# A transformer trunk in float32: the MLP as one loop over both matrices, or as two stages with seven block products for the first

## The chip, the cores and the metric
One of the cores of a Trainium2 chip runs the kernel; nothing else runs beside it. The metric is device time of one execution in microseconds (us). The engines named below are PE (TensorE, matmuls), DVE (VectorE), ACT (ScalarE), POOL (GpSimd), and SP, on whose queue most transfers between DRAM and the core's SBUF memory are issued. Matmul results arrive in PSUM, which has eight banks of 128 x 512 float32.

## The reference
Two layers over 1024 latent tokens and 256 context tokens, 1024 features wide. Each layer: norm and modulation, three mixers (attention, Fourier, long convolution), one output projection, and then an MLP, which alone the change touches (with the projection before it):

```
x = x + g1 * heads_out(att_x, px, hy, w_out[l])
x = x + g2 * sq_relu_mlp(modulate(rms_norm(x, norm2_g[l]), sh2, sc2), w_mlp1[l], w_mlp2[l])
...
def sq_relu_mlp(h, w1, w2):
    return jnp.square(jax.nn.relu(h @ w1)) @ w2
```

`w1` is 1024 x 4096 and `w2` 4096 x 1024. Layer 0 does this for the context tokens too, with the same weights; layer 1 for the latents alone. Shift, scale and gate of layer 1 come from a product of a vector with a 1024 x 6144 matrix (`wmod`).

## The kernel before
Activations lie with features on the 128 partitions and tokens along the free axis, so x is eight tiles `xT` of 128 x 1024 (and `xC` of 128 x 256 for the context). Tokens are worked in chunks: 512, 512 and, in layer 0, 256 of the context.

Every float32 operand is cut into a high part (a cast on ACT) and a low part (the difference), and a product is three matmuls into one PSUM bank, high x high, high x low, low x high (`mm3`, lines 137 to 140). Weights come in raw tiles of 128 x 1024 (512 KB, `wload`, lines 122 to 128, into a ring of three to seven slots) and are cut by `wsplit` (lines 130 to 135): cast on ACT (L133), subtraction on POOL (L134). The parts `wh` and `wl` have two buffers each. Activations are cut by `split_sb` (L147, L148): cast on ACT, subtraction on DVE or, where it is asked for, POOL.

The order of the work: the program names the operations in sequence, each engine keeps its own queue, and background generators (`spawn(rate, gen)`) are advanced by `tick()` in the loops. A scheduler then reorders what is independent, so the order on an engine is not the text's.

After the attention the output projection runs as two calls of `half_k`: weights of four contraction tiles at a time, output tiles in four groups `mg` of two, and each PSUM result added onto x by `resid` (L1117, DVE reads PSUM and x). The second call goes chunk by chunk, and in layer 1 the last chunk is split into two of 256. As a chunk of x becomes final, its squares are summed (L199 on ACT, L201 on DVE), `rstd_diag` (L218, L219) and `rstd_rows` (L225 on PE, L227) turn the sum into a row, the norm's factor in every partition, and `norm_gen` makes the scaled and shifted operand's parts `hh` and `hl` (L243 to L245).

`mlp` then alternates: for each of eight groups `hc`, four weight tiles of `w1` times all chunks, relu and square (L1179 on ACT, L1180 on DVE), the parts `uh` and `ul` kept in SBUF, and then `half_k` with `w2` onto x. Beside layer 0's MLP `late_modulation` loads the last 48 tiles of layer 1's `wmod` and runs 64 dot products over 128 x 1024 on DVE (L161), spread by a rate of 0.45 per tick.

## Time and profile before

| what | value |
|---|---|
| time, three runs | 3266.49 us median (3265.97, 3266.49, 3275.97) |
| profiled execution, span from first to last instruction | 3268.1 us |
| PE busy | 3096.4 us, 16238 matmuls, 95 % of the span |
| PE weight loads, beside the matmuls | 2584.0 us, 79 % |
| DVE busy | 1830.7 us, 56 % |
| ACT busy | 1204.9 us, 37 % |
| POOL busy | 1049.0 us, 32 % |
| mean granted clock of PE | 0.978 of full |
| DMA | 326 MB, mean 100 GB/s |

The times and the profile are of different executions. For the profiled one only the span is known, which lies 1.6 us above the median. Busy matmul time is modelled at its ends, and neighbours overlap, so the price of one matmul is read from how many fit into a stretch, not from a mean duration. A wait is put down to the event that came last.

### The profile page before, as it was taken

The numbers are of one execution on the slowest core, as the hardware profiler recorded it, in microseconds if no ns is written. First come the engines' busy times: TensorE is split into PE (matmuls) and PEld (weight loads), VectorE is DVE, ScalarE is ACT, GpSimd is POOL, SyncE is SP. The second block draws the span as 40 slices with busy tenths as digits, with TensorE's granted clock in tenths as the row PEclk, the third lists the DMA queues.
The fourth block names the chain that finished last, engine by engine and source line by source line (L and its number), as shares of the span: only waits on it lengthen the run. The fifth ranks groups of instructions, "written<-read, shape, count | busy, mean of one in ns | idle before, by whom it ended". The sixth has DMA issues, their size and how long they took to land. (4 is left out here: it accounts for less than half of the span.)

```text
span 3268.1 us, 41676 instructions
## 1 busy us (share of the span) xinstructions
PE 3096.4 (95%) x16238; PEld 2584.0 (79%) x16238; DVE 1830.7 (56%) x2943; ACT 1204.9 (37%) x2167; POOL 1049.0 (32%) x676
## 2 busy tenths in 40 slices
PE   5999998999999999999999999998998999999997
PEld 1787886887778888888887887787877788888886
DVE  7985679886664444332226535779867322222226
ACT  4324475674331112112214424576654222222113
POOL 6334337542411111111113224347434222222223
PEclk8999998999999999999999998999999999999999
DMA  6454662434222232221113224653242111111113
GB/s 238 157 187 120 200 179 80 128 91 148 84 72 84 91 103 91 78 71 38 35 39 123 94 86 131 218 135 81 68 166 90 39 52 46 46 51 46 51 47 110
DMA packets 121036, 326.29 MB, mean 100 GB/s; under 512 B 32838, under 2 KB 44263, under 8 KB 120584
## 3 DMA queue, kind: packets, MB, share of 16 engines
q1 hardware_dynamic: 107832, 281.88, 27.7%
q0 software_dynamic: 9504, 34.67, 3.5%
q10 hardware_dynamic: 3504, 7.08, 0.6%
q8 instruction: 128, 2.10, 0.3%
q14 instruction: 68, 0.56, 0.1%
HBM read 270.11 MB, written 53.48 MB: 99 GB/s over the span
## 5 line engine op out<-in xcount | busy, mean ns | idle before, releaser
L134 POOL TENSOR_TENSOR wl<-wr,wh 128x1024 fp32r<-128x1024 f32 (+1 forms) x214 | 519.2, 2427 | 1641.8 <-ACT wh L133 1623.9
L133 ACT CAST wh<-wr 128x1024 fp32r<-128x1024 f32 (+1 forms) x214 | 221.5, 1035 | 962.0 <-PE pso L139 680.2
L140 PE MATMUL pso<-uh,wl 128*128 128x512 f32 (+1 forms) x1312 | 484.1, 369 | 4.2 <-POOL wl L134 4.2
L138 PE MATMUL pso<-uh,wh 128*128 128x512 f32 (+1 forms) x1312 | 487.5, 372 | 0.6 <-ACT wh L133 0.6
L1117 DVE SCALAR_TENSOR_TENSOR xT<-pso,modc,xT 128x512 f32<-128x512 f32 (+1 forms) x336 | 241.8, 722 | 438.4 <-PE pso L140 438.4
L138 PE MATMUL psm<-hh,wh 128*128 128x512 f32 (+1 forms) x1280 | 477.4, 374 | 4.3 <-ACT hh L244 4.2
L139 PE MATMUL pso<-ul,wh 128*128 128x512 f32 (+1 forms) x1312 | 480.7, 366 | 0.0
L140 PE MATMUL psm<-hh,wl 128*128 128x512 f32 (+1 forms) x1280 | 472.9, 370 | 3.5 <-POOL wl L134 3.5
L139 PE MATMUL psm<-hl,wh 128*128 128x512 f32 (+1 forms) x1280 | 474.9, 371 | 0.5 <-DVE hl L245 0.4
L1180 DVE SCALAR_TENSOR_TENSOR rl<-psm,rl 128x256 f32<-128x256 f32 (+1 forms) x160 | 101.7, 636 | 460.0 <-ACT rl L1179 459.9
L140 PEld LDWEIGHTS pso<-uh,wl 128*128 128x128 f32 x1312 | 247.8, 189 | 51.5 <-POOL wl L134 5.1
L139 PEld LDWEIGHTS pso<-ul,wh 128*128 128x128 f32 x1312 | 249.5, 190 | 45.2 <-issue 0.5
L138 PEld LDWEIGHTS pso<-uh,wh 128*128 128x128 f32 x1312 | 248.0, 189 | 44.5 <-ACT wh L133 0.8
L138 PEld LDWEIGHTS psm<-hh,wh 128*128 128x128 f32 x1280 | 241.7, 189 | 49.0 <-ACT hh L244 6.5
L140 PEld LDWEIGHTS psm<-hh,wl 128*128 128x128 f32 x1280 | 241.5, 189 | 47.9 <-POOL wl L134 3.9
L139 PEld LDWEIGHTS psm<-hl,wh 128*128 128x128 f32 x1280 | 241.6, 189 | 43.9 <-DVE hl L245 2.5
L1017 POOL TENSOR_SCALAR p<-p,st 128x1280 f32<-128x1280 f32 (+1 forms) x144 | 182.8, 1269 | 268.0 <-DVE st L1012 122.4
L144 DVE TENSOR_TENSOR pt<-pst,pt 128x512 fp32r<-128x512 f32 x328 | 214.4, 680 | 11.7 <-ACT pt L143 10.5
L143 ACT CAST pt<-pst 128x512 fp32r<-128x512 f32 x328 | 181.8, 589 | 86.3 <-PE pst L1038 68.2
L139 PE MATMUL psi<-hl,wh 128*128 128x512 f32 (+1 forms) x536 | 198.4, 370 | 5.8 <-POOL hl L241 3.4
L138 PE MATMUL psi<-hh,wh 128*128 128x512 f32 (+1 forms) x536 | 200.9, 376 | 1.8 <-ACT hh L244 1.1
L140 PE MATMUL psi<-hh,wl 128*128 128x512 f32 (+1 forms) x536 | 197.2, 368 | 3.2 <-POOL wl L134 3.2
(338 smaller groups left out, 6121.0 us busy)
## 6 DMA issues: line engine op xcount, KB each, us to landing
wr<-w SPq DMA_DIRECT2D x144, 512.0 KB, 3.5
wr<-wmod SPq DMA_DIRECT2D x64, 512.0 KB, 3.3
tb<-ftab POOLq DMA_DIRECT2D x34, 512.0 KB, 4.7
wm<-wmod SPq DMA_DIRECT2D x32, 512.0 KB, 3.6
wr<-wout SPq DMA_DIRECT2D x32, 512.0 KB, 3.6
wr<-win SPq DMA_DIRECT2D x26, 512.0 KB, 3.3
d_qk<-qk SPq DMA_DIRECT2D x18, 640.0 KB, 5.3
qk<-d_qk SPq DMA_DIRECT2D x18, 640.0 KB, 6.2
```

The lines of the kernel that those rows point to most:

```text
L133: S.copy(hi[:, :n], t[:, :n])
L134: G.tensor_tensor(lo[:, :n], t[:, :n], hi[:, :n].bitcast(F32), op=ALU.subtract)
L138: T.matmul(ps, lhsT=lh, rhs=rh, start=first, stop=False)
L139: T.matmul(ps, lhsT=lh, rhs=rl, start=False, stop=False)
L140: T.matmul(ps, lhsT=ll, rhs=rh, start=False, stop=last)
L143: S.copy(hi, ps)
L144: V.tensor_tensor(lo, ps, hi.bitcast(F32), op=ALU.subtract)
L1017: G.tensor_scalar(pr, pr, st[:, 5:6], 1.0, op0=ALU.mult, op1=ALU.mult)
L1117: V.scalar_tensor_tensor(x, ps[:, : c1 - c0], g, x, op0=ALU.mult, op1=ALU.add)
L1180: V.scalar_tensor_tensor(r[:, :n], ps[:, :n], 0.0, r[:, :n], op0=ALU.max, op1=ALU.mult)
```

## The change
The MLP becomes two stages, `up` and `down`, with the activations u = relu(.)^2 in DRAM (`d_u`) between them.

In `up` the latents' first matrix is worked as 2 x 2 blocks: the weights of two tiles A1 and A2 (a11, a12, a21, a22, half a tile each), the tokens' two halves and the two halves of the features. Seven products of four contraction tiles replace eight. Their token operands are b11, b21 (first half of the tokens), b22 and the four sums t1 to t4, made once a layer by `norm_blocks`; their weight operands are A1, `r41` (its halves a11 + a12 - a21 - a22 and a21 + a22), `r32` (a21 + a22 - a11 and a11 - a21) and half of A2, made for each of 16 periods j. Results are joined on DVE, passed through relu and square on ACT and stored. `top` makes the first two products p1 and p2, which need the first half of the tokens alone: for the first four (layer 0) or five (layer 1) periods they are made ahead, with their sum parked in DRAM (`d_s1`), while the second half's operands are made. The context keeps eight plain products per tile.

In `down` the tiles of u are loaded, cut again (low part on POOL) and multiplied with `w2` by `half_k` as before. x is stored to `d_x2` after the projection and loaded back in `down`. Layer 1's last chunk of the projection is one of 512. The late modulation starts inside `down`, from its second group, at a rate of 2.2.

```diff
+AHEAD = 4, 5
...
-        def mlp(l, xT, h, pool, psp, last_passes):
...
+            def second(acc):
+                yield
+                r = yield from rows(acc)
+                V.tensor_tensor(sh4, modc[:, l, 0, 3 * ND + 4 : 3 * ND + 8], modc[:, l, 0, 3 * ND : 3 * ND + 4], op=ALU.subtract)
+                for k in range(4):
+                    scaled(4 + k, xs1[4 + k], r)
+                    parts("b22", k, 4 + k, xs1[4 + k])
+                    if k % 2:
+                        yield
+                for k in range(4):
+                    scaled(k, xs1[k], r)
+                    t = nt("t1")
+                    V.tensor_tensor(t, xs1[k], xs0[k], op=ALU.subtract)
+                    split_sb(*ops["t1"][k], t, G)
+                    yield
+                    t3 = nt("t3")
+                    V.scalar_tensor_tensor(t3, xs1[4 + k], sh4[:, k : k + 1], xs1[k], op0=ALU.add, op1=ALU.subtract)
+                    split_sb(*ops["t3"][k], t3, G)
+                    t2 = nt("t2")
+                    V.scalar_tensor_tensor(t2, xs1[4 + k], shift(4 + k), t, op0=ALU.add, op1=ALU.subtract)
+                    split_sb(*ops["t2"][k], t2, G)
+                    yield
+                    t4 = nt("t4")
+                    V.scalar_tensor_tensor(t4, xs0[4 + k], shift(4 + k), t2, op0=ALU.add, op1=ALU.subtract)
+                    split_sb(*ops["t4"][k], t4, V)
...
+        def up(l, ops, hx, opening, psp, chain):
+            def prod(w, at, name):
+                ps = psp.tile([128, 512], F32, tag="ps", name="psm")
+                for k in range(4):
+                    ks = slice(at + k * 128, at + k * 128 + 128)
+                    mm3(ps, w[0][:, ks], w[1][:, ks], *ops[name][k], k == 0, k == 3)
+                return ps
...
+            def block(m, t0, x, y):
+                c = room("c")
+                V.tensor_tensor(c, x, y, op=ALU.add)
+                S.activation(c, c, AF.Relu)
+                out(c, m, t0)
...
+            def top(j, raw):
+                w = wsplit(raw, 1024)
+                p1 = prod(w, 0, "b11")
+                p2 = prod(w, 512, "b21")
+                s1 = room("s1")
+                S.copy(s1, p1)
+                block(2 * j, 0, s1, p2)
+                context(w, 2 * j)
+                return s1
+            for g in chain[:-1]:
+                drain(g)
+            for j in range(AHEAD[l]):
+                nc.sync.dma_start(out=d_s1[j], in_=top(j, wload(a["w1"][l, 2 * j], 1024)))
+                for _ in range(4):
+                    tick()
+            drain(chain[-1])
+            for j in range(16):
+                A1, A2 = (wload(a["w1"][l, 2 * j + u], 1024) for u in range(2))
+                a11, a12, a21, a22 = A1[:, :512], A1[:, 512:], A2[:, :512], A2[:, 512:]
+                if j < AHEAD[l]:
+                    s1 = room("s1")
+                    nc.sync.dma_start(out=s1, in_=d_s1[j])
+                else:
+                    s1 = top(j, A1)
+                r41 = wroom()
+                G.tensor_tensor(r41[:, 512:], a21, a22, op=ALU.add)
+                V.tensor_tensor(r41[:, :512], a11, a12, op=ALU.add)
+                V.tensor_tensor(r41[:, :512], r41[:, :512], r41[:, 512:], op=ALU.subtract)
+                w = wsplit(r41, 1024)
+                if j == 0:
+                    pool = opening()
+                    slots((pool, "wr2", 4))
+                    ring["at"] = 2
+                r32 = wroom()
+                V.tensor_tensor(r32[:, 512:], r41[:, 512:], a11, op=ALU.subtract)
+                V.tensor_tensor(r32[:, :512], a11, a21, op=ALU.subtract)
+                p3 = prod(w, 0, "b22")
+                p5 = prod(w, 512, "t1")
+                tick()
+                w = wsplit(r32, 1024)
+                p7 = prod(w, 0, "t3")
+                p6 = prod(w, 512, "t2")
+                V.tensor_tensor(s1, s1, p6, op=ALU.add)
+                u3 = room("u3")
+                V.tensor_tensor(u3, s1, p7, op=ALU.add)
+                V.tensor_tensor(s1, s1, p5, op=ALU.add)
+                block(2 * j + 1, 512, u3, p5)
+                block(2 * j, 512, s1, p3)
+                tick()
+                w = wsplit(A2, 1024)
+                p4 = prod(w, 512, "t4")
+                block(2 * j + 1, 0, u3, p4)
+                context(w, 2 * j + 1)
+                tick()
+        def down(l, xT, chunks, pools, psp, late, last_passes):
+            te = chunks[-1][1] if chunks[-1][1] > SEQ else SEQ
+            def load(hc, us):
+                for j in range(4):
+                    u = {c0: tuple(pools[hc % 2].tile([128, c1 - c0], F32R, tag=f"u{c1 - c0}", bufs=16 if c1 - c0 == 512 else 8,
+                                             name=f"u{x}") for x in "hl") for c0, c1, _ in chunks}
+                    w = pools[0].tile([128, TT], F32, tag="ur", bufs=3, name="ur")
+                    nc.sync.dma_start(out=w[:, :te], in_=d_u[hc * 4 + j][:, :te])
+                    for c0, (hi, lo) in sorted(u.items()):
+                        split_sb(hi, lo, w[:, c0 : c0 + hi.shape[1]], G)
+                    us.append(u)
+                    yield
...
+            us = [[] for _ in range(8)]
+            drain(load(0, us[0]))
+            back = load_back()
+            next(back)
+            spawn(1, back)
+            for hc in range(7):
+                g = load(hc + 1, us[hc + 1])
+                spawn(1, g)
+                if hc == 1:
+                    spawn(2.2, late)
+                half_k(l, 5, a["w2"][l, hc], us[hc], chunks, xT, psp)
+                drain(g)
+            now_ = us[7]
+            last_passes(now_)
...
-            h2 = new_h(PM, cself if last else cself[2:] + cself[:2])
-            crow = PM.tile([128, 2, 1024], F32, name="crow")
-            norms = spawn(1)
-            halves = [(c0, c1, cc, hs, todo) for cc, ce, hs, todo in h2
-                      for c0, c1 in (((cc, cc + 256), (cc + 256, ce)) if last and cc else ((cc, ce),))]
-            for i, (c0, c1, cc, hs, todo) in enumerate(halves):
-                acc, dg = (crow[:, i % 2, u * 512 : u * 512 + c1 - c0] for u in range(2))
-                part = [tuple(x[:, c0 - cc : c1 - cc] for x in p) for p in hs]
-                half_k(l, 2, a["wout"][l, 0], cat2, [(c0, c1, cc)], xT, psp,
-                       after=sums_by(acc, [xcol(xT, j, c0, c1) for j in range(ND)]))
-                g = norm_gen(l, 1, xT, c0, c1, part, acc, dg)
-                todo.append(g)
-                spawn(1, g)
+            hx = None if last else new_h(PM, CHUNKS[2:])[0][2]
+            acc = [PM.tile([128, 512], F32, name=f"nacc{i}") for i in range(2)]
+            dg = PM.tile([128, 512], F32, name="ndg")
+            sh4 = PM.tile([128, 4], F32, name="sh4")
+            norms = norm_blocks(l, [x[0][:, :512] for x in xT], [x[0][:, 512:] for x in xT], ops, acc, dg, sh4)
+            todo = ([] if last else [(CHUNKS[2], acc[1], norm_gen(l, 1, xT, SEQ, TT, hx, acc[1][:, :CTX], dg[:, :CTX]))]) + \
+                [(CHUNKS[i], acc[i], norms[i]) for i in range(2)]
+            for (c0, c1), ac, g in todo:
+                add = sums_by(ac[:, : c1 - c0], [xcol(xT, j, c0, c1) for j in range(ND)])
+
+                def after(mg, c0=c0, c1=c1, add=add):
+                    add(mg)
+                    for j in (2 * mg, 2 * mg + 1):
+                        nc.sync.dma_start(out=d_x2[j][:, c0:c1], in_=xcol(xT, j, c0, c1))
+
+                half_k(l, 2, a["wout"][l, 0], cat2, [(c0, c1, c0)], xT, psp, after=after)
+                spawn(2, g)
...
+            up(l, ops, hx, opening, psp, [g for _, _, g in todo])
+            slots()
+            wctx.close()
+            PMc.close()
+            xT = alloc_x(xctx, l + 1 if not last else DEPTH)
+            uctx = ExitStack()
...
                 if not last:
                     def late_modulation():
-                        for _ in range(3):
-                            yield
+                        crow = pools[0].tile([128, 2, 1024], F32, name="crow")
                         load_crow(crow)
                         yield from modulation(1, crow, (1, 0, 2, 4, 3, 5), lambda s: (0, 1) if s < 2 else (0,))
 
-                    spawn(0.45, late_modulation())
+                    late = late_modulation()
...
-                mlp(l, xT, h2, pool, psp, last_passes)
+                slots((pools[0], "wr2", 2))
+                down(l, xT, chs, pools, psp, late, last_passes)
```

The order in three places. First DVE, layer 1, where the normed operands are made. Before, each tile of the first half's operand takes a scaled row (L243) and a low part (L245):

```order
L243 SCALAR_TENSOR_TENSOR ht_22445<-xT0_21552,gsc_63,rstd_22443 128x512
L243 SCALAR_TENSOR_TENSOR ht_22449<-xT1_21553,gsc_63,rstd_22443 128x512
L243 SCALAR_TENSOR_TENSOR ht_22453<-xT2_21554,gsc_63,rstd_22443 128x512
L245 SCALAR_TENSOR_TENSOR hl0_0_22082<-ht_22445,modc_62,hh0_0_22081 128x512
L245 SCALAR_TENSOR_TENSOR hl0_1_22084<-ht_22449,modc_62,hh0_1_22083 128x512
L243 SCALAR_TENSOR_TENSOR ht_22457<-xT3_21555,gsc_63,rstd_22443 128x512
L245 SCALAR_TENSOR_TENSOR hl0_2_22086<-ht_22453,modc_62,hh0_2_22085 128x512
```

Now, in the second half (L1177 scaled row, L1182 low part of a shifted operand, L1211 to L1222 the sums, L155 their low parts, L1250 the joining of two products, `xT0` to `xT7` the tiles of x):

```order
L1177 SCALAR_TENSOR_TENSOR xT0_22182<-xT0_22182,gsc_63,rstd_23201 128x512
L1177 SCALAR_TENSOR_TENSOR xT1_22183<-xT1_22183,gsc_63,rstd_23201 128x512
L1211 TENSOR_TENSOR t1_23217<-xT0_22182 128x512
L1182 SCALAR_TENSOR_TENSOR b22l3_23117<-xT7_22189,modc_62,b22h3_23116 128x512
L1215 SCALAR_TENSOR_TENSOR t3_23221<-xT4_22186,sh4_22733,xT0_22182 128x512
L1218 SCALAR_TENSOR_TENSOR t2_23225<-xT4_22186,modc_62,t1_23217 128x512
L1177 SCALAR_TENSOR_TENSOR xT2_22184<-xT2_22184,gsc_63,rstd_23201 128x512
L1222 SCALAR_TENSOR_TENSOR t4_23229<-xT4_22186,modc_62,t2_23225 128x512
L1177 SCALAR_TENSOR_TENSOR xT3_22185<-xT3_22185,gsc_63,rstd_23201 128x512
L1250 TENSOR_TENSOR c_23267<-s1_23265,psm_23252 128x512
L1211 TENSOR_TENSOR t1_23274<-xT1_22183 128x512
L155 TENSOR_TENSOR t4l0_23143<-t4_23229,t4h0_23142 128x512
```

For two tiles of features there are eight operations, each with two inputs in SBUF, where four stood, and among them the joins of the first periods (L1250, one input in PSUM).

Second, POOL in layer 1's first stage. Before, one row per weight tile:

```order
L134 TENSOR_TENSOR wl_24911<-wr_24908,wh_24910 128x1024
L134 TENSOR_TENSOR wl_24981<-wr_24978,wh_24980 128x1024
```

Now, in a period (L141 the low part of a weight pair, of A1, r41, r32 and A2 in turn; L1290 the sum a21 + a22, a period ahead):

```order
L1290 TENSOR_TENSOR wr_24178<-wr_24139 128x512
L141 TENSOR_TENSOR wl_23998<-wr_23993,wh_23997 128x1024
L141 TENSOR_TENSOR wl_24039<-wr_24034,wh_24038 128x1024
L141 TENSOR_TENSOR wl_24072<-wr_24042,wh_24071 128x1024
L141 TENSOR_TENSOR wl_24116<-wr_23995,wh_24115 128x1024
L1290 TENSOR_TENSOR wr_24322<-wr_24283 128x512
```

For two weight tiles there are four weight pairs and one addition.

Third, SP's queue at the end of layer 0's first stage. Before, at that place in the MLP, only weights are loaded:

```order
L127 DMA wr_9786<-w1 128x1024
L127 DMA wr_9824<-wmod 128x1024
L127 DMA wr_9898<-wmod 128x1024
L127 DMA wr_9904<-w1 128x1024
L127 DMA wr_9974<-wmod 128x1024
```

Now (L1246 stores of u, L1329 its loads, L1339 x loaded back; `d_u31` is the last tile of u, `d_u1` to `d_u3` belong to the first group of the second stage):

```order
L1246 DMA d_u31_134<-c_12310 128x512
L1329 DMA ur_12409<-d_u0_103 128x1280
L1246 DMA d_u30_133<-c_12315 128x512
L1246 DMA d_u31_134<-c_12337 128x512
L1246 DMA d_u31_134<-c_12367 128x256
L1329 DMA ur_12423<-d_u1_104 128x1280
L1329 DMA ur_12437<-d_u2_105 128x1280
L1329 DMA ur_12451<-d_u3_106 128x1280
L1339 DMA xT0_12381<-d_x20_95 128x1024
```

and some rows further on

```order
L1329 DMA ur_12599<-d_u6_109 128x1280
L1329 DMA ur_12647<-d_u7_110 128x1280
L134 DMA wr_12711<-w2 128x1024
L134 DMA wr_12801<-w2 128x1024
```

The loads of u1 to u3 stand behind the context's last store, and two of the first group's weight tiles behind the second group's tiles of u.

## Rows read from the trace of the kernel before

**Rows 1.** The head of the page: the span, each engine's busy time (share of the span, instructions), and PE and its granted clock in 40 equal slices, each digit in tenths.
```profile
span 3268.1 us, 41676 instructions
...
PE 3096.4 (95%) x16238; PEld 2584.0 (79%) x16238; DVE 1830.7 (56%) x2943; ACT 1204.9 (37%) x2167; POOL 1049.0 (32%) x676
...
PE   5999998999999999999999999998998999999997
...
PEclk8999998999999999999999998999999999999999
```

**Rows 2.** Busy time of each engine in stretches: stretch in us, its length, then busy us of PE, of its weight loads, of DVE, ACT and POOL (with instructions), the mean granted clock of PE, the busy share of the DMA engines, GB/s. 820 to 960 is layer 0's step from the output projection to the MLP and 2480 to 2560 layer 1's; 960 to 1740 lies in layer 0's MLP and 2600 to 3200 in layer 1's.
```profile
820.00:840.00 20.00, 19.51 (x133) 17.76 (x131) 8.78 (x13) 4.56 (x7) 6.04 (x4) 1.00 0.27 79
840.00:860.00 20.00, 17.41 (x87) 14.36 (x87) 14.54 (x15) 8.75 (x14) 10.06 (x5) 1.00 0.32 106
...
880.00:900.00 20.00, 18.00 (x98) 14.80 (x97) 16.93 (x23) 8.32 (x14) 7.43 (x4) 1.00 0.28 83
900.00:920.00 20.00, 17.20 (x74) 12.45 (x74) 17.50 (x30) 11.43 (x21) 0.00 (x0) 0.94 0.23 73
920.00:940.00 20.00, 18.00 (x97) 14.83 (x96) 12.29 (x18) 12.16 (x17) 5.17 (x2) 0.97 0.16 56
960.00:1740.00 780.00, 780.00 (x4033) 663.48 (x4032) 297.47 (x471) 146.34 (x224) 138.05 (x56) 1.00 0.22 71
2480.00:2500.00 20.00, 18.37 (x134) 16.72 (x133) 17.24 (x20) 10.51 (x16) 11.84 (x6) 1.00 0.37 111
2500.00:2520.00 20.00, 12.37 (x86) 11.67 (x85) 19.41 (x23) 10.97 (x18) 8.31 (x4) 0.88 0.35 111
2520.00:2540.00 20.00, 14.15 (x54) 11.44 (x54) 15.79 (x35) 8.66 (x20) 2.34 (x1) 0.78 0.12 42
2540.00:2560.00 20.00, 18.40 (x72) 14.66 (x73) 10.86 (x22) 8.37 (x16) 4.82 (x2) 0.91 0.12 33
2600.00:3200.00 600.00, 600.00 (x2599) 488.33 (x2598) 166.06 (x216) 121.92 (x166) 130.57 (x55) 1.00 0.16 48
```

**Rows 3.** PE's waits between 2480 and 2570 us: what waited, for which engine's operation; us in total, times, longest. L225 spreads the norm's row (from L219 on DVE) over the partitions.
```profile
PE psn L225 <- DVE crow L219: 10.3, 2, 8.6
PE pso L140 <- POOL wl L134: 3.6, 4, 2.0
```

**Rows 4.** The page's costliest groups: the first of the three matmuls of a product in the MLP's first matrix; busy us, mean ns of one, idle before it.
```profile
L138 PE MATMUL psm<-hh,wh 128*128 128x512 f32 (+1 forms) x1280 | 477.4, 374 | 4.3 <-ACT hh L244 4.2
```

**Rows 5.** DVE in time order around the same step of layer 1: start us, us, line and operation, out<-in, in brackets the idle time before and its cause. A row with x3 is three operations in a row. L201 adds squares (two SBUF tiles), L1117 adds a PSUM tile onto x, L243 scales x by the norm's row (two SBUF tiles).
```profile
2482.50 0.69 DVE L201 TENSOR_TENSOR crow<-crow,sq 128x512 f32<-128x512 f32 x1 [0.76 <-ACT sq L199]
...
2484.23 0.48 DVE L1117 SCALAR_TENSOR_TENSOR xT<-pso,modc,xT 128x256 f32<-128x256 f32 x1 [0.37 <-PE pso L140]
2484.63 2.06 DVE L201 TENSOR_TENSOR crow<-crow,sq 128x512 f32<-128x512 f32 x1
...
2491.59 2.33 DVE L201 TENSOR_TENSOR crow<-crow,sq 128x256 f32<-128x256 f32 x1 [0.48 <-ACT sq L199]
...
2502.45 2.08 DVE L243 SCALAR_TENSOR_TENSOR ht<-xT,gsc,rstd 128x512 f32<-128x512 f32 x3
...
2505.77 2.84 DVE L243 SCALAR_TENSOR_TENSOR ht<-xT,gsc,rstd 128x512 f32<-128x512 f32 x1
```

**Rows 6.** POOL's groups by shape: the low part of a weight pair, and of a 512-wide tile; count, busy us, mean ns, idle before.
```profile
L134 POOL TENSOR_TENSOR wl<-wr,wh 128x1024 fp32r<-128x1024 f32 x204 | 502.4, 2464 | 1630.1 <-ACT wh L133 1612.2 <-PE pso L140 17.8
...
L148 POOL TENSOR_TENSOR heho<-eo,heho 128x512 fp32r<-128x512 f32 x18 | 25.3, 1405 | 24.7 <-ACT heho L147 24.7
```

**Rows 7.** POOL in time order, same columns as rows 5.
```profile
2483.74 2.39 POOL L134 TENSOR_TENSOR wl<-wr,wh 128x1024 fp32r<-128x1024 f32 x1 [3.21 <-ACT wh L133]
...
2491.27 2.37 POOL L134 TENSOR_TENSOR wl<-wr,wh 128x1024 fp32r<-128x1024 f32 x1 [2.20 <-ACT wh L133]
...
2505.63 2.43 POOL L134 TENSOR_TENSOR wl<-wr,wh 128x1024 fp32r<-128x1024 f32 x1 [4.88 <-ACT wh L133]
```

**Rows 8.** ACT's groups by shape: the high part of a weight pair, and of a 512-wide tile.
```profile
L133 ACT CAST wh<-wr 128x1024 fp32r<-128x1024 f32 x204 | 214.0, 1049 | 952.3 <-PE pso L139 680.2 <-PE psm L139 190.6 <-PE psi L139 36.1
...
L147 ACT CAST uh<-rl 128x512 fp32r<-128x512 f32 x128 | 79.4, 621 | 94.0 <-DVE rl L1180 94.0
```

**Rows 9.** PE in time order, three matmuls of the output projection that waited for the low part of a weight pair, in brackets for how long.
```profile
2486.19 0.39 PE L140 MATMUL pso<-cat,wl 128*128 128x256 f32 x1 [0.36 <-POOL wl L134]
...
2498.28 0.39 PE L140 MATMUL pso<-cat,wl 128*128 128x256 f32 x1 [0.62 <-POOL wl L134]
...
2508.11 0.48 PE L140 MATMUL pso<-cat,wl 128*128 128x256 f32 x1 [2.00 <-POOL wl L134]
```

**Rows 10.** DMA issues: what, count, KB each, median us from issue to landing.
```profile
wr<-w SPq DMA_DIRECT2D x144, 512.0 KB, 3.5
...
qk<-d_qk SPq DMA_DIRECT2D x18, 640.0 KB, 6.2
```

**Rows 11.** DVE's groups by shape: the residual update, and one pass of the modulation (L161).
```profile
L1117 DVE SCALAR_TENSOR_TENSOR xT<-pso,modc,xT 128x512 f32<-128x512 f32 x304 | 227.0, 748 | 436.6 <-PE pso L140 436.6
...
L161 DVE SCALAR_TENSOR_TENSOR junk<-wr,crow 128x1024 bf16<-128x1024 f32 x80 | 109.9, 1384 | 21.9 <-DMA wr<-wmod 16.7 <-ACT crow L152 4.6 <-POOL r L201 0.6
```

More of the change, by code (lines that the diff above doesn't have):

```diff
@@ L74, in trunk @@
         d_v = tc.dram_tile([10, 128, 512], F32, name="d_v")
+        d_x2 = [tc.dram_tile([128, TT], F32, name=f"d_x2{m}") for m in range(ND)]
+        d_u = [tc.dram_tile([128, TT], F32, name=f"d_u{m}") for m in range(32)]
+        d_s1 = [tc.dram_tile([128, 512], F32, name=f"d_s1{m}") for m in range(max(AHEAD))]
         d_kh = {(l, s): tc.dram_tile([2, 128, 2048 if s == 0 else 512], F32, name=f"d_kh{l}{s}")
@@ new lines, in down, with load_back @@
+        def down(l, xT, chunks, pools, psp, late, last_passes):
[9 more added lines that the diff above has]
+                    us.append(u)
+                    yield
+            def load_back():
+                for m in range(ND):
+                    for x, (s0, s1) in zip(xT[m], ((0, SEQ), (SEQ, TT))):
+                        if x is not None:
+                            nc.sync.dma_start(out=x, in_=d_x2[m][:, s0:s1])
+                    if m % 2:
+                        yield
+            us = [[] for _ in range(8)]
[12 more added lines that the diff above has]
+            last_passes(now_)
@@ L1207, in side_job @@
                     yield from hyena_apply(l, stream, pool, psp)
-            xs[:] = alloc_x(xctx, l + 1)
+            pools = [c.enter_context(pool_(f"P{u}F{l}", "right")) for c, u in zip(xctx, ("X", "XC"))]
+            xs[:] = [(pools[0].tile([128, SEQ], F32, name=f"xT{j}"),
+                      pools[1].tile([128, CTX], F32, name=f"xC{j}") if l < DEPTH - 1 else None) for j in range(ND)]
             load_x(l, xs)
@@ L1318, in first @@
                     pools.append(more.enter_context(pool_(f"PAU{l}")))
-                    spawn(0.72 if last else 0.88, side_job(l, psp, xctx, xT, rctx, raw))
+                    spawn(0.72 if last else 0.88, side_job(l, psp, fctx, xT, rctx, raw))
                 attention(l, heads, room, hpool[0], pools, psp, first())
@@ new lines, in trunk, with opening @@
+            fctx[1].close()
+            PT = PMc.enter_context(pool_(f"PT{l}"))
+            ops.update({name: operand(PT, name) for name in ("b22", "t1", "t3", "t2", "t4")})
+            wctx = ExitStack()
+            def opening():
+                fctx[0].close()
+                return wctx.enter_context(pool_(f"PA{l}", "right"))
+            up(l, ops, hx, opening, psp, [g for _, _, g in todo])
[3 more added lines that the diff above has]
+            xT = alloc_x(xctx, l + 1 if not last else DEPTH)
@@ L1364, in last_passes @@
                     finish()
-                    PMc.close()
+                    slots()
+                    uctx.close()
                     norms = spawn(1)
```

78 lines of the change are left out of this document (49 added, 29 removed).

## The prediction
> **What bounds the kernel now.** I read the page's busy times first, then stretches, then single operations. TensorE (PE) is busy 95 % of the span at a granted clock near full, the next engine 56 % [rows 1]: the time is PE's work plus the places where PE stands still. The stretch table says where those are. Inside both MLPs there are none: 780.00 us busy of 780.00 in layer 0, 600.00 of 600.00 in layer 1, clock 1.00, the 2.4 GHz level [rows 2]. So a matmul taken out there shortens the run by its whole length, as long as its operands still arrive in time. The idle time lies at the step from output projection to MLP. In layer 0 PE lacks 0.5 + 2.6 + 2.0 + 2.8 + 2.0 = 9.9 us between 820 and 960, and 0.94 and 0.97 of clock in two rows add 1.6: 11.5 us lost. In layer 1 it lacks 1.6 + 7.6 + 5.9 + 1.6 = 16.7 us between 2480 and 2560, and clocks of 0.88, 0.78 and 0.91 add 6.3: 23 us lost [rows 2]. The longest wait there, 8.6 us, is for the norm's row on DVE; weight pairs on POOL cost 3.6 us in four waits [rows 3]. The change rebuilds exactly this step.
>
> **What it takes away.** One 512-wide matmul, back to back, takes 600/2599 = 0.2308 us [rows 2]; the mean of 374 ns in the page's group overlaps its neighbours and is not the price [rows 4]. A layer's first matrix over the latents is 32 weight tiles x 8 x 3 x 2 chunks = 1536 of these; seven block products make it 16 x 7 x 4 x 3 = 1344. 192 fewer in each layer: 2 x 192 x 0.2308 = 88.6 us. In layer 1 two 256-wide chunks of the output projection become one 512-wide: 780 us with 4033 matmuls, a third of them 256 wide, gives (780 - 2689 x 0.2308)/1344 = 0.119 us for a narrow one [rows 2], so 96 x (2 x 0.119 - 0.2308) = 0.7. The order agrees: PE has 480 matmuls fewer, 384 and 96. Gain: 89.3 us.
>
> **The opening of each layer's first stage.** New work stands between the norm and PE: the second half's scaled rows, the sums t1 to t4 and their splits. From the first scaled row of the second half to t1's last part, DVE has 31 operations (8 scaled rows, 4 low parts of b22, 4 t1, 9 of t2 to t4, 3 low parts of t4, 2 for r41, a join) of 0.69 (three in 2.08, unhindered [rows 5]) = 21.4 us; POOL has ten 512-wide subtractions of 1.4, four weight splits of 2.46 and an addition of 1.4 [rows 6] = 25.3 us. What hides it is the work done ahead: p1 and p2 are 24 x 0.2308 = 5.5 us a weight pair, five pairs in layer 1 = 27.7; in layer 0 the context adds 24 x 0.119 = 2.9, and four pairs make 33.8.
>
> Side by side the two engines would need 25 us and fit. The trace says they do not run side by side. A DVE addition of two SBUF tiles takes 0.69 with POOL idle, and 2.06 and 2.33 where it began in a POOL split that started 0.9 and 0.3 us earlier; a scaled row stretched to 2.84 [rows 5, 7]. A DVE operation that reads PSUM kept its 0.48 inside the same POOL split [rows 5]. So I add them: 46.7 us. This is the rule of the Trainium skill, "SBUF — State Buffer", section "SBUF: two separate sides": DVE with two SBUF inputs and POOL hold one port pair as an exclusive lock for a whole instruction. The trace agrees, 2.06 against 0.69; by the rule the opening takes 46.7 us, without it 25.3.
>
> Layer 1: 46.7 - 27.7 = 19 short, then the first half's norm ahead of p1 and p2, for which the nearest row is the 8.6 us wait [rows 3], then the next pair's cast and split, 1.05 + 2.46 = 3.5 [rows 6, 8], and 2 for a fallen clock: 33 against 23 before, a cost of 10. Layer 0: 12.9 + 8.6 + 3.5 = 25 against 11.5, a cost of 13.5. Together I take **24**. Bounds: with no blocking 8.6 + 3.5 remain in each layer, 24 against 34.5, a gain of 10; with further collisions as in the 2.00 us wait for a weight pair [rows 9], 36.
>
> **The steady first stage.** Each period uses four weight pairs. PE spends 5.5 us on three and only 2.8 on A2's half pair, while hi and lo parts have two buffers: the pair behind A2 can be prepared only from where A2 starts. That takes 1.05 + 2.46 [rows 6, 8], with hand-overs 3.7, against 2.8 + 0.46 until the first matmul that needs the low part: 0.4 to 0.5 us in each of layer 1's 15 periods, the size of the 0.36 and 0.62 us waits of the trace, where two such pieces lie equally close [rows 9]. **7.5** in all; in layer 0 the context (2.9 us) covers it. Bounds: 0, and 2.0 a period [rows 9], 30. The sums on DVE, the squares on ACT, the stores and POOL's 11 us of a 19 us period lie beside PE's work; if that cover goes, POOL is late first.
>
> **The step between the stages.** The activations must come back from DRAM. On SP's queue the loads of u1, u2 and u3 stand behind the last context store. From PE's last matmul of the first stage: relu and square 1.2, store 2 (an estimate below the 3.5 us of 512 KB), loads of 640 KB 6.2 [rows 10], cast 0.62, then POOL's parts, 1.4 each, tile after tile: about 14 us until u3 is there. Meanwhile PE has 37 matmuls = 8.5 us that need only earlier tiles. Loss 6 and 2.5 of clock: 8.5. Layer 1 has no context store and two early tiles: 3.5. Sum **12**; bounds 5 (all but the last tile early) and 22 (nothing beside it). Behind these loads stand the x tiles, u4 to u7, and only then the second matrix's third and fourth weights; u6 and u7 wait for POOL to free a raw tile, near 23 us, so those weights land about 27 us after the step, some 5 us before PE needs them. A gap on POOL reaches PE through them.
>
> **Late modulation, moved.** It was spread over layer 0's MLP and cost nothing (PE 780 of 780 [rows 2]). Now 64 of its passes run in some nine weight groups of the second stage, 9 x 13.9 = 125 us of PE. DVE needs 64 x (1.384 + 0.08) = 94 for them, at a mean that holds its share of blocking, and 34 residual updates of 0.748, 25 [rows 11]: 119 of 125. Tight, but eight PSUM banks, some 18 us of PE, cover a late update. **5**; bounds 0, and 20 if POOL's 50 us there (nine weight splits, 28 of u parts) exclude them wholly: 94 + 50 - 125. The 48 weight loads stand between the u loads on SP and land in 3.5 each [rows 10]; nobody else waits.
>
> **Nothing** for: storing and reloading x (they stand behind other work; PE needs x only when a PSUM bank fills), s1 in DRAM, the re-splitting of u in the second stage (POOL 22 of 56 us).
>
> Sum: 89.3 - 24 - 7.5 - 12 - 5 = 40.8 us, from the profiled 3268.1 [rows 1] to 3227.3. The median of the runs, 3266.5, lies 1.6 lower: **3225.7**. About 0.3 %, 9.8 us, is what a measurement of this kernel can tell from no change.
>
> **Rivals.**
> (a) The opening is hidden: hand-overs let POOL and DVE alternate where neither is needed next, so the opening gains 10. Costs 14.5: 3191.7. For: 25 us each fits under 27.7. Against: [rows 5, 7].
> (b) **Slower.** Blocking in every period: DVE's four additions of two SBUF tiles a period for r41 and r32 fall into the split of the pair behind A2, and PE waits 2.0 us there, as once in the trace [rows 9], in 31 periods: 62 instead of 7.5. With the rest of the step costs somewhat up (opening 36), 115: 3292; with the opening as taken, 3280. It decides from (89.3 - 41)/31 = 1.6 us a period. For: that wait exists. Against: it needs the collision every time, and of the four waits for weight pairs [rows 3] the other three sum to 1.6; the sums for r41 and r32 stand well ahead in DVE's order.
> (c) Step and modulation at their upper ends: 22 + 20 + 24 + 7.5 = 73.5: 3250.7. For: one queue carries stores, loads and weights; DVE's 119 of 125. Against: PSUM slack.
> (d) Fewer matmuls did not arise: excluded by PE's order, which is shorter by 480.
>
> **Chances.** Forecast 0.52, (a) 0.21, (c) 0.16, (b) 0.11. The range leaves out 0.1 on each side: from 3187, just under (a), to 3264, past (c) and short of (b). Within 0.3 % (3256.7 to 3276.3) lie the worse end of (c) and the mild end of (b): 0.08. Slower 0.09; faster 0.83.
>
> **What would show it.** The MLP stretch in layer 1 at 2.31 us for ten matmuls, as now. In the opening PE waiting on t1 and weight pairs, 25 to 33 us a layer, DVE operations of 2 us beside POOL's; none of these, and (a) holds. In layer 1's first stage 0.5 us for POOL's low part once a period; 2 us is (b). At the step one wait for a u part of 6 us. In the modulation PE without waits; waits for a PSUM bank are (c). A gain above 100 us, or PE's matmul price changed, would make the argument wrong.

## The result and the profile after

The changed kernel takes 3285.8 us in the median against 3270.7 for the kernel before, both over ten runs: ratio 1.0051, 95 % interval 1.0037 to 1.0065. One of the ten executions of the changed kernel, 6194.8 us at a granted clock of 1.00, was in a slow state and is not in the ratio. The change makes the kernel slower, by half a per cent; the forecast was 3225.7 and faster. The head of its page, as [rows 1] of before:

```profile
span 3282.8 us, 42701 instructions
...
PE 3041.8 (93%) x15756; PEld 2518.2 (77%) x15756; DVE 1943.5 (59%) x2976; ACT 1367.7 (42%) x2425; POOL 1490.0 (45%) x952
...
PE   5999998999889999899999999998999799989998
...
PEclk8999998999989999999999998999999899999998
```

Two differences carry it. PE's busy time fell by 3096.4 - 3041.8 = 54.6 us, not by the 89.3 of the matmuls taken out: 34.7 came back, since the matmuls that are left take longer. PE's idle time rose from 171.7 to 241.0: 69.3. 69.3 + 34.7 - 89.3 = 14.7, the difference of the spans (3282.8 - 3268.1). Where both arose, by stretches (columns as in [rows 2]; opening, steady first stage, step between the stages and modulation of layer 0, then opening, steady stage and step of layer 1):

```profile
895.80:971.70 75.90, 58.40 (x260) 46.18 (x259) 59.32 (x65) 34.11 (x57) 39.37 (x21) 0.84 0.29 97
971.70:1337.00 365.30, 357.57 (x1865) 302.26 (x1863) 118.38 (x162) 149.10 (x243) 161.25 (x72) 1.00 0.30 96
1337.00:1382.00 45.00, 33.58 (x151) 26.55 (x152) 7.85 (x12) 18.87 (x33) 32.35 (x27) 0.90 0.94 353
1382.00:1502.00 120.00, 112.83 (x554) 94.24 (x553) 115.10 (x162) 19.25 (x31) 64.24 (x32) 0.97 0.66 228
...
2518.50:2592.10 73.60, 53.84 (x187) 39.79 (x186) 62.01 (x66) 34.27 (x53) 43.36 (x22) 0.81 0.34 111
2592.10:2887.90 295.80, 280.09 (x1169) 220.87 (x1167) 137.20 (x159) 124.53 (x180) 159.91 (x71) 0.98 0.33 104
2887.90:2932.90 45.00, 35.43 (x139) 27.58 (x139) 9.48 (x14) 15.46 (x25) 27.87 (x20) 0.89 0.84 310
```

The loss of a stretch is its length less 0.2308 us for each 512-wide and 0.119 for each 256-wide matmul in it, the two prices of the prediction. For layer 1's steady stage that is 295.8 - 1167 x 0.2308 = 26.5, or 26.4 with the price not rounded. Opening here includes the output projection ahead of it.

| loss, us | before | after | cost | forecast |
|---|---|---|---|---|
| opening, layer 0 | 20.3 | 40.8 | 20.5 | 13.5 |
| opening, layer 1 | 26.4 | 33.9 | 7.5 | 10 |
| steady first stage, layers 0 and 1 | 1.9 | 10.4 + 26.4 | 34.9 | 7.5 |
| step, layers 0 and 1 | none | 15.5 + 13.1 | 28.6 | 12 |
| modulation | none | 12.2 | 12.2 | 5 |
| the rest of both MLPs | 19.6 | 23.0 | 3.4 | 0 |

107 us against a gain of 89.3, which is 3 us more than the 14.7 by which the span grew: the stretches outside the table, which the change leaves alone, were 3 to 4 us shorter in this execution. The openings came out about as summed (28 against 24). The steady stage, the step and the modulation together cost three times their terms (75.7 against 24.5).

What a bad period of the steady stage looks like: POOL, DVE and PE of the changed kernel, in time order, columns as in [rows 5].

```profile
2654.85 1.80 POOL L1290 TENSOR_TENSOR wr<-wr 128x512 f32<-128x512 f32 x1
2656.61 5.24 POOL L141 TENSOR_TENSOR wl<-wr,wh 128x1024 fp32r<-128x1024 f32 x2
```
```profile
2656.68 2.90 DVE L1292 TENSOR_TENSOR wr<-wr 128x512 f32<-128x512 f32 x1 [1.18 <-POOL wr L1290]
```
```profile
2659.09 0.50 PE L147 MATMUL psm<-b11h,wl 128*128 128x512 f32 x1 [1.18 <-POOL wl L141]
...
2678.99 0.50 PE L147 MATMUL psm<-b11h,wl 128*128 128x512 f32 x1 [0.23 <-POOL wl L141]
```

The sum a21 + a22 (L1290) stands in POOL's queue ahead of two weight pairs, and L1292, which waits for it, collides with the first of them (2.90 instead of 0.69). The pair behind A2, which has the least slack, is last: 1.18 us of waiting. A period later nothing stands in front, and the wait is 0.23. PE's waits for low parts in layer 1's steady stage:

```profile
PE psm L147 <- POOL wl L141: 15.3, 17, 2.4
```

Seven of these waits are longer than 1 us (1.18 to 2.35). Four are of the kind just shown, at the pair of A1 or of r41; in three of the four the sum had itself waited 3.5 to 3.9 us at the head of POOL's queue for a raw weight tile to land. The other three, at the pairs of r32 and A2, come another way, with POOL idle:

```profile
2788.23 2.32 DVE L1292 TENSOR_TENSOR wr<-wr 128x512 f32<-128x512 f32 x1
```
```profile
2792.98 0.63 ACT L1251 ACTIVATE c<-c 128x512 f32<-128x512 f32 x1 [5.47 <-DVE c L1250]
...
2796.73 1.04 ACT L140 CAST wh<-wr 128x1024 fp32r<-128x1024 f32 x1
```
```profile
2797.85 4.79 POOL L141 TENSOR_TENSOR wl<-wr,wh 128x1024 fp32r<-128x1024 f32 x2 [7.85 <-ACT wh L140]
```
```profile
2800.31 0.50 PE L147 MATMUL psm<-t3h,wl 128*128 128x512 f32 x1 [1.75 <-POOL wl L141]
```

DVE's sum L1292 collides with a weight pair on POOL and takes 2.32 us. The joins (L1250) and the last sum for r32, behind it on DVE, come about 1.6 us later for it (2.32 - 0.69, an estimate). ACT works off their relus and squares (L1251, L1245) ahead of the cast of r32, POOL stands idle 7.85 us until that cast, and PE waits 1.75.

### The profile page after: what moved, and what is told of

It is laid out like the page before. It is cut to its first block, busy times and chain, and to the rows that moved or that the text cites. A ratio compares the mean times of both kernels' runs of the same rounds, so it can differ in the third digit from the quotient of the medians.

```text
span 3282.8 us, 42701 instructions
## 1 busy us (share of the span) xinstructions
PE 3041.8 (93%) x15756; PEld 2518.2 (77%) x15756; DVE 1943.5 (59%) x2976; ACT 1367.7 (42%) x2425; POOL 1490.0 (45%) x952
## 5 line engine op out<-in xcount | busy, mean ns | idle before, releaser
L141 POOL TENSOR_TENSOR wl<-wr,wh 128x1024 fp32r<-128x1024 f32 (+1 forms) x274 | 666.1, 2433 | 1117.0 <-ACT wh L140 1115.1
L140 ACT CAST wh<-wr 128x1024 fp32r<-128x1024 f32 (+1 forms) x274 | 283.8, 1036 | 850.8 <-PE pso L146 357.4
L155 POOL TENSOR_TENSOR ul<-ur,uh 128x512 fp32r<-128x512 f32 (+1 forms) x160 | 205.2, 1313 | 46.7 <-ACT uh L154 41.4
L1063 PE MATMUL pv<-pt,v 128*128 128x256 f32 x656 | 170.2, 295 | 14.8 <-DVE pt L151 13.5
L1064 PE MATMUL pv<-pt,v 128*128 128x256 f32 x656 | 165.9, 290 | 5.7 <-DVE pt L151 5.6
L1291 DVE TENSOR_TENSOR wr<-wr 128x512 f32<-128x512 f32 x32 | 38.3, 1198 | 219.7 <-POOL wl L141 116.8
L1045 PE MATMUL pst<-ident,p 128*128 128x128 f32 x1024 | 147.3, 278 | 22.0 <-DVE pt L151 10.0
L1011 DVE TENSOR_REDUCE st<-sx 128x1 f32<-128x1024 f32 x128 | 155.7, 1216 | 15.3 <-PE sx L147 14.7
L1017 ACT ACTIVATE p<-sx,st,acol 128x1024 f32<-128x1024 f32 x128 | 153.7, 1201 | 0.0
```

What stands on the lines that cost most here:

```text
L140: S.copy(hi[:, :n], t[:, :n])
L141: G.tensor_tensor(lo[:, :n], t[:, :n], hi[:, :n].bitcast(F32), op=ALU.subtract)
L155: (eng or V).tensor_tensor(lo, src, hi.bitcast(F32), op=ALU.subtract)
L1063: T.matmul(pv[:, :256], lhsT=vt[:, kt, :], rhs=th, start=j == 0, stop=False)
L1064: T.matmul(pv[:, :256], lhsT=vt[:, kt, :], rhs=tl, start=False, stop=j == n - 1)
```

## The experiments

The line numbers of these kernels differ by a few from those above; the losses are worked out as in the table, the opening without the projection ahead of it.

**The sums and pairs apart from the two stages.** two_plain keeps the two stages and undoes the block products.

```diff
-                p3 = prod(w, 0, "b22")
-                p5 = prod(w, 512, "t1")
...
+            for m in range(32):
+                w = top(m) if m >= AHEAD[l] else wsplit(wload(a["w1"][l, m], 1024), 1024)
...
+                half(w, m, 512, ("t1", "b22"))
```

> The two stages with u in DRAM kept, the block products undone: the first stage makes eight plain products per pair of weight tiles, without the sums t1 to t4, r41 and r32. PE gets 384 matmuls more, 88.6 us. Theory 1 (the cost of the first stage is the preparation of the weight pairs and sums): the loss of the steady first stage, 10.4 us in layer 0 and 26.4 in layer 1, goes to about 2, the openings lose 15 less together, the step between the stages (12 and 12.6) and the modulation (16) stay: about 3283 + 89 - 35 - 15 = 3322 us, which is 50 above the kernel before. Rival (the traffic through DRAM and the queue on SP slow the first stage): the steady loss stays, 3350 or more.

3292.6 us, ratio to before 1.0079 (1.0066 to 1.0092). Opening and steady stage of layer 0, then of layer 1:

```profile
894.80:944.90 50.10, 42.72 (x212) 35.63 (x211) 27.18 (x34) 23.86 (x39) 10.17 (x5) 0.90 0.40 140
944.90:1354.20 409.30, 409.30 (x2105) 347.87 (x2103) 0.00 (x0) 124.46 (x206) 76.80 (x32) 1.00 0.28 85
...
2533.90:2572.80 38.90, 35.17 (x140) 26.96 (x140) 27.70 (x34) 21.33 (x33) 12.45 (x5) 0.91 0.44 141
2572.80:2897.50 324.70, 324.70 (x1409) 264.19 (x1407) 0.00 (x0) 101.94 (x151) 77.40 (x32) 1.00 0.32 100
```

Steady stage: no idle time, with the same stores to DRAM. So its loss belongs to the block products, not to the traffic. The openings lose 13.9 and 8.6 instead of 28.7 and 32.3: the sums t1 to t4 and r41 cost 38.5 there, where 15 was expected. Together 38.5 + 36.8 = 75 of the 88.6 us saved went back, and the changed kernel's steps lose some 8 more than here (28.6 against 11.1 and 9.2); by the ratios (1.0079 and 1.0051) 9 us remain of the block products. Two stages by themselves, with what moved along with them, cost 0.8 %, 26 us, over the kernel before.

**The weight sums, and POOL's queue.**

```diff
-                r41 = wroom()
-                G.tensor_tensor(r41[:, 512:], a21, a22, op=ALU.add)
...
-                w = wsplit(r41, 1024)
+                w = wsplit(A2, 1024)
```

> The sums of the weights are left out: A2 and A1 stand where r41 and r32 stood, so the products are other ones, of the same number. Four weight pairs per period remain, the five additions go. Theory 1a (the additions block POOL's low parts or stand before them in POOL's queue): the steady loss falls from 36.8 us to about 10 and the openings lose some 5 less: 3250 us. Rival 1b (two buffers for four pairs are too few, whatever else runs): steady loss nearly as before, 3275 to 3280.

3250.8 us (0.9944 to 0.9969). Layer 1's steady stage, and PE's waits from 2600 to 2864:

```profile
2586.90:2864.30 277.40, 274.16 (x1169) 217.99 (x1167) 67.90 (x105) 124.48 (x179) 136.38 (x57) 1.00 0.33 111
```
```profile
PE psm L147 <- POOL wl L141: 3.0, 14, 0.2
```

Layer 0's steady loss is gone, layer 1's falls from 26.4 to 8.1: four pairs with two buffers cost 0.2 us of waiting once a period, as long as no sum stands among them. The sums make the other 18. But 3.0 us of waits lose 8.1 at a clock of 1.00: around a 0.2 us wait PE loses some 0.5. The waits of the later periods come 19.90 us apart, and the 84 matmuls between them would take 19.39 back to back; the matmul behind a wait takes 0.50 instead of 0.39, and its overlap with its neighbours is lost.

```diff
-                G.tensor_tensor(r41[:, 512:], a21, a22, op=ALU.add)
+                V.tensor_tensor(r41[:, 512:], a21, a22, op=ALU.add)
```

> One edit: the sum a21 + a22 is made on DVE, not on POOL. Theory 1a-queue (that sum waits for a late weight tile at the head of POOL's queue and the low parts stand behind it): PE's waits for low parts in layer 1's steady stage fall from 15.1 us to about 5, time by 8 to 15, to about 3272. Rival 1a-lock (DVE's additions hold the port): DVE has one addition more to hold it with, no gain, 3280 to 3290.

3274.8 us (1.0016 to 1.0034), steady losses 9.2 and 20.0. The sum out of POOL's queue gains 0.26 %, some 8 us, the 7.6 of these stages. Its place in the queue has a share, but most of the loss is still there: layer 1's waits for low parts fell from 15.3 us to 11.9, not to 5, and theory 1a-queue alone does not carry it. All five waits above 1 us that are left there (1.22 to 1.76) are of the second kind, with a DVE sum of 2.30 to 2.33 us ahead of the joins and POOL idle for ACT's cast.

```diff
+                    pairs["slots"] = [(P0, "", 2), (P0, "", 2), (pool, "3", 1)]
```

> A third buffer for the high and low parts of a weight pair in the first stage (and five instead of six joining tiles, for room). If the steady loss is a pair that is made too late because its buffer comes free late, by whatever 2 us it is then delayed, it is hidden by the 5 us that a buffer more gives: steady loss from 36.8 to 5, time 3250. If the raw weight tiles or POOL's throughput limit, the loss stays: 3280.

3252.1 us (0.9953 to 0.9977), faster than before. The steady stages:

```profile
972.30:1327.80 355.50, 355.50 (x1865) 302.67 (x1863) 121.36 (x162) 148.97 (x242) 159.75 (x71) 1.00 0.30 100
2581.00:2854.50 273.50, 271.81 (x1169) 218.97 (x1167) 140.70 (x159) 124.72 (x179) 161.69 (x71) 1.00 0.35 115
```

0.6 and 4.2 lost instead of 36.8, with every sum still there, and DVE's collisions too (its two sums that read `r41[:, 512:]` take 1.76 and 1.32 us in the mean in layer 1, 1.66 and 1.81 in the changed kernel). The openings lose 31.3 and 33.8, a little more than without the buffer. The step of the prediction that failed is shown by this run and no_weight_sums: the sums, by POOL's queue or by the way over DVE and ACT, delay a pair by 1 to 2 us, and with only two buffers that becomes a wait.

**The opening.**

```diff
-                    split_sb(*ops["t1"][k], t, G)
+                    split_sb(*ops["t1"][k], t, V)
```
(and t2 and t3 likewise)

> One edit: the low parts of t1, t2 and t3 are made on DVE instead of POOL, 12 operations a layer. Theory 2 (DVE and POOL exclude each other in the opening, so their times add): a part costs 0.69 on DVE against 1.3 to 1.7 on POOL, the sum falls by 7 to 12 us a layer; opening losses 28.7 and 32.3 go to about 21 and 24, time by about 15, to 3270. Rival 2 (the engines run side by side and the longer one decides): DVE's 21 us become 29, the opening loses as much or some 7 more a layer: 3286 to 3300.

3276.9 us (1.0017 to 1.0040). Openings 21.6 and 29.3: 7.1 and 3.0 less. Work moved onto the busier engine shortened the opening, against rival 2; the size in layer 1 is below what was expected. The Trainium skill ("SBUF — State Buffer", "SBUF: two separate sides") says that of a DVE operation with two SBUF inputs and a POOL operation, whichever starts first holds their port pair for its whole instruction, so both should be seen to stretch. The trace agrees: in the changed kernel's opening of layer 1 the parts on POOL and the sums on DVE (mean ns) are 1720 and 1874, where 1.3 us (the 16 parts of u at layer 1's step, 1262 to 1306 ns) and 0.69 us are their unhindered times:

```profile
L155 POOL TENSOR_TENSOR t3l<-t,t3h 128x512 fp32r<-128x512 f32 x4 | 6.9, 1720 | 2.6 <-ACT t3h L154 2.6
```
```profile
L1211 DVE TENSOR_TENSOR t<-xT 128x512 f32<-128x512 f32 x4 | 7.5, 1874 | 0.0
```

```diff
-AHEAD = 4, 5
+AHEAD = 6, 8
```

> One edit: 6 and 8 instead of 4 and 5 first product pairs are made ahead, 17 us more of PE work over the opening in each layer. Theory 2 (the opening is short of cover): in each layer the loss falls by 17 less the weight splits that the new pairs put onto POOL (2.46 each, 5 and 7.4 us): about 10 a layer, time 3265. Rival (the weight pair of r41 is late because POOL and ACT serve the pairs ahead first): the opening only moves, loss unchanged within 4 us, and the extra stores and loads cost a little: 3285 to 3292.

3294.4 us (1.0063 to 1.0090). The openings lose 25.1 and 29.1, only 3.4 less each, as the rival had it, and the steady stages lose 16.1 and 39.8, 19 us more together, which neither side had.

**Modulation and step.**

```diff
-                    spawn(2.2, late)
+                    spawn(0.8, late)
...
+                    w = pools[0].tile([128, TT], F32, tag="ur", bufs=3, name="ur")
                     u = {c0: ...
-                    w = pools[0].tile([128, TT], F32, tag="ur", bufs=3, name="ur")
```

> On top of three weight-pair buffers: the late modulation at a rate of 0.8 instead of 2.2, and in the second stage the raw tiles of u allocated ahead of their parts, so that they lie over operands that are free earlier. Theory 3 (64 passes in 131 us with POOL's u parts exclude each other and a weight pair's low part comes 4.5 us late): spread over twice the time, layer 0's stretch after the step loses 2 instead of 14. Theory 4 (the first u tile waits for the memory of the last operand): its wait of 7.2 and 6.2 us falls to about 3, two layers 8. Together 3252 - 12 - 8 = 3232. Rivals: the modulation's loss is its loads' share of the queue, unchanged; the first u tile waits for its own transfer, unchanged: 3250.

3245.0 us (0.9915 to 0.9944). The modulation's stretch of layer 0:

```profile
1370.80:1490.80 120.00, 120.00 (x624) 102.15 (x623) 92.39 (x135) 20.89 (x32) 58.51 (x32) 1.00 0.52 180
```

No loss, instead of 12.2 in the changed kernel and 14.0 in three_pairs, on which this one is built. In the changed kernel the wait was this (DVE and POOL by shape, then PE's waits, 1382 to 1502):

```profile
L168 DVE SCALAR_TENSOR_TENSOR junk<-wr,crow 128x1024 bf16<-128x1024 f32 x55 | 87.0, 1602 | 0.0
```
```profile
L155 POOL TENSOR_TENSOR ul<-ur,uh 128x512 fp32r<-128x512 f32 x16 | 35.0, 2210 | 7.1 <-ACT uh L154 7.1
```
```profile
PE pso L147 <- POOL wl L141: 6.2, 2, 4.5
```

DVE was not late, it made POOL late: parts of 1.3 us took 2.21, and a weight pair stood behind them. At the lower rate the same stretch has 40 of DVE's passes instead of 55, and the parts take 1.84. The run holds both edits, so that the rate did it, and not the order of the tiles, is argued from these rows. Theory 4 fell: the steps lost 12.1 and 13.1, against 12.5 and 13.6 in three_pairs.

```diff
-                    nc.sync.dma_start(out=w[:, :te], in_=d_u[hc * 4 + j][:, :te])
+                    for s0, s1 in ((0, 512), (512, te)) if hc == 0 else ((0, te),):
+                        nc.sync.dma_start(out=w[:, s0:s1], in_=d_u[hc * 4 + j][:, s0:s1])
...
-                        split_sb(hi, lo, w[:, c0 : c0 + hi.shape[1]], G)
+                        split_sb(hi, lo, w[:, c0 : c0 + hi.shape[1]], V if hc == 0 else G)
```
(with the t parts on DVE as above)

> The kernel before this one with the low parts of t1 to t3 on DVE, and at the step between the stages u's first four tiles loaded as a piece of 512 and the rest, with their low parts on DVE. If theories 2 to 4 hold and add: 3232 - 15 (openings) - 6 (low parts at the step on the idle DVE, 0.7 instead of 1.3 to 1.4 each) = 3211. If the opening's rival holds: 3235 or more.

3251.7 us (0.9932 to 0.9963), 7 us more than without, though the two intervals overlap a little, and far from the 3211: steps 14.6 and 15.5, openings 26.5 and 31.7 (30.6 and 33.6 without), and layer 1's steady stage 17.1 instead of 4.3. So a third buffer does not hide every delay: in the longest wait of that stage, 4.1 us, POOL's sum had waited 4.2 for a raw weight tile, with two pairs behind it. Why that grows when the t parts move to DVE stays open. The miss led to SP's queue in the changed kernel, at the end of layer 1's first stage (last product at 2887.6), and its waits from 2875 to 2890:

```profile
2888.64 0.33 SPq L134 DMA_DIRECT2D wr<-w  x1
2889.07 0.86 SPq L1329 DMA_DIRECT2D ur<-d_u  x2
```
```profile
SPq L134 <- POOL wl L141: 14.7, 2, 10.2
```

A weight load waits 10.2 us for the raw slot of A2, and u's first load, whose data has long been stored, waits behind it.

```diff
                 slots((pools[0], "wr2", 2))
+                ring["at"] = 2
```

> On top of pairs_slow_mod one line: the second stage's first weights take the raw slots that come free with the second stage, not the ring's slot of the last weight tile of the first. Theory 5 (on SP's queue a weight load waits 10.2 us for that slot, and in layer 1 u's first load stands behind it): now no such load stands ahead of u's first in layer 1, PE's wait for the first part of u falls from 6.7 to about 3 there, the step loses 13.1 - 4 = 9, layer 0 (where u's first load stands behind a store) about the same; time 3245 - 4 = 3241. Rival 4 (the load waits for the memory of the last operand, whatever stands ahead): unchanged, 3245.

3262.3 us (0.9972 to 0.9992). SP's queue, and PE's waits from 2850 to 2880:

```profile
2843.56 0.38 SPq L1335 DMA_DIRECT2D ur<-d_u  x1
```
```profile
PE pso L149 <- ACT wh L144: 16.4, 1, 16.4
...
```

u's first load now goes 11 us ahead of the last product (2854.5), as theory 5 says, but the wait moved to the first weight, which stands behind x and u: steps 23.2 and 19.8, and the time is 17 us above that of pairs_slow_mod, where 4 less was expected.

> The kernel beside it with the low parts of t1 to t3 on DVE as well, without the split loads of all_edits. If the 9 us that those parts gave alone add: 3241 - 8 = 3233, the openings losing 22 and 30. If the rise of layer 1's steady loss in all_edits (17 against 4) came with the parts on DVE and not with the split loads: 3245.

3270.0 us (0.9995 to 1.0021): that kernel with the t parts on DVE, above both expectations, which had counted on 3241 without the parts. Steady loss in layer 1 17.3 again, so it came with those parts and not with the split loads; openings 24.6 and 31.7. In these two kernels with a third buffer, what the parts gain in the openings is lost again in that stage.

```diff
+                ring["at"] = 1
```

> Like u_before_weights, on top of pairs_slow_mod, but the second stage's first weight keeps the ring's slot and only the second and third take the slots that come free with the stage. In u_before_weights u's first load went out 11 us before the last product of layer 1's first stage, instead of 1.4 us after it, and PE then waited 16 to 18 us for a weight. Theory 5 (one queue: what stands ahead decides which of the two is late): with the first weight early and one load fewer ahead of u, the step of layer 1 loses 8 to 10 instead of 13.1, layer 0 12, time 3240. Rival (any slot taken from the ring makes a weight late): second weight waits as in u_before_weights, step 20, 3255.

3256.7 us (0.9949 to 0.9975): PE waits 3.9 for u in each layer, and 7.6 and 5.2 for a weight; steps 23.2 and 18.5. The rival was right: in both orders tried, the load put forward delayed another. An order of the queue that keeps both early was not found, and what the step must cost stays open.

**Slack and cover together.** AHEAD = 6, 8 as in more_ahead, on top of pairs_slow_mod.

> 6 and 8 product pairs ahead, as in more_ahead, on top of pairs_slow_mod (three weight-pair buffers). In more_ahead the openings lost 3.5 less each, and the steady stages 6 and 13 more. Theory 1 (a period whose p1 and p2 are made ahead has 13.8 us of PE for three pairs and one addition and so the least slack, which a third buffer mends): the steady stages stay at about 1 and 5, openings 27 and 30: 3245 - 7 = 3238. Rival (the stores and loads of the parked sums cost the steady stage): it loses 6 and 13 more here too: 3260.

3233.3 us, ratio to before 0.9901 (0.9886 to 0.9917), the fastest. Opening and steady stage, layers 0 and 1:

```profile
893.20:979.70 86.50, 74.00 (x356) 60.91 (x355) 63.95 (x66) 41.89 (x70) 43.31 (x23) 0.90 0.35 113
979.70:1322.20 342.50, 340.75 (x1769) 289.00 (x1767) 128.79 (x160) 141.10 (x229) 157.03 (x70) 1.00 0.31 102
2488.90:2577.00 88.10, 70.59 (x260) 53.27 (x259) 72.77 (x72) 43.01 (x66) 53.84 (x27) 0.86 0.41 134
2577.00:2834.80 257.80, 255.65 (x1097) 205.31 (x1095) 149.92 (x153) 116.68 (x167) 153.30 (x67) 1.00 0.37 120
```

Openings 22.7 and 30.4, steady stages 4.3 and 4.9 instead of more_ahead's 16.1 and 39.8. Against pairs_slow_mod (0.5 and 4.3) that is 3.8 and 0.6 more, not the rival's 6 and 13, so parked sums cost the steady stage little; periods without p1 and p2 have less work over their pairs, and a third buffer mends that.

## Why the prediction was wrong

- **What bounds the kernel, and the gain**: right. PE has 480 matmuls fewer (482 in the two traces' counts), and a matmul costs 0.2308 us in a stretch without idle time after the change as well (324.70 us for 1407 in two_plain).
- **The opening**: right in mechanism and near in sum, 28 against 24. Blocking is shown by t_parts_on_dve, and the share of the sums by two_plain. That the sum is so near is luck: it was too low in layer 0 by 7 and too high in layer 1 by 2.5, the norm's 8.6 us in each layer came out as waits of 3.3 us at most, and the longest waits, 5.1 and 7.4, were for casts of weight pairs (r32 and r41), whose sums stand on DVE among the blocked operations. The cover in layer 0 adds up to 33.6, not 33.8, which changes nothing.
- **The steady first stage, the step that failed.** The term was 0.4 to 0.5 us in 15 periods, 7.5, and nothing in layer 0; the stage lost 34.9 more than before. For a period without sums the term holds: no_weight_sums lost 8.1 in layer 1 and nothing in layer 0, though with a wait of 0.2 us a period and the rest around it. What failed is that the sums on DVE, the squares on ACT and POOL's work were put at nothing, as lying beside PE's work. Waits of 1.2 to 2.4 us, the size of rival (b)'s, came in 7 of layer 1's 15 periods, and in layer 0 as well, mostly in its first periods, whose p1 and p2 had been made ahead. Only three of the seven were at the pair behind A2, where (b) had put them. The prediction looked at collisions of one pair; it left out that the sum on POOL stands in the same queue, that a collision on DVE delays the joins and with them ACT's next cast, and that a period without p1 and p2 has no cover from them. It put (b) at 0.11 since the sums stand well ahead in DVE's order; the time at which they run, not their place, decides. That the measured 3285.8 lies between (b)'s 3280 and 3292 is chance: (b) had 62 us here, where 34.9 came, and the step and the modulation made up the difference.
- **Waits priced at their length.** Layer 1's steady loss of 26.4 has 15.7 of waits in it. The rest is the clock, a mean of 0.98 in that stretch, and by the rows of no_weight_sums an estimated 0.3 us of restart for each wait. The 34.7 us that came back over the run are these two together, which the trace does not part; the granted clock is 0.967 against 0.978. The prediction gave the clock 2 us in an opening, in which it now stands at 0.81, and 2.5 at one step.
- **The step**: 28.6 against 12. The term reckoned with the last tile, u3; what came late was u's first tile, 7.2 and 6.2 us. In layer 1 its load stood behind a weight load that waited 10.2 us for its slot, in layer 0 behind a store of u, issued at 1335.52 with the load at 1336.68. That queue was named, but for other loads. Which order would cost less was not found.
- **The modulation**: 12.2 against 5, within its bounds of 0 to 20. The cover that was named, PSUM, held; the wait came through POOL's queue.
- **The range** ended at 3264: all four terms missed to the same side. DVE's and POOL's blocking of each other is in three of them, the opening, the steady stage and the modulation, while the chances treated them as apart; the step's miss is SP's queue.

## What to carry to other kernels

Where engines in program order feed PE through two buffers, price a new operation not by its busy time but by the slack of the pieces that stand behind it, on its own engine and on those that wait for it, and count a wait as its length plus the restart plus what a lower granted clock costs around it. A third buffer for that piece was worth 0.86 % here (ratio 0.9965 against 1.0051), where taking one operation out of the queue brought 0.26 %. Put terms that hang on the same late engine up and down together when the range is set.

## What was not expected of the hardware

A wait of 0.2 us cost PE about 0.5 us of throughput at full clock (8.1 us for some 15 of them). DVE's blocking works both ways: POOL's 512-wide parts rose from 1.3 to 2.21 us beside 55 DVE passes over 128 x 1024, whose mean rose to 1.60 from the 1.384 of [rows 11]. The granted clock, a mix of the levels 2.4 and 1.2 GHz, was lowest where waits of some us followed one another: a mean of 0.84 and 0.81 in the openings and 0.90 and 0.89 at the steps, and 1.00 in the steady stage of layer 0, where nine waits of 0.2 to 1.8 us stood mostly 18 us or more apart.
